# A chunk's running sum ordered behind the present step of the RWKV scan, and the solution's values copied on chip instead of loaded again

## The chip, the cores and the metric

The kernel runs on one core of a Trainium2 chip. The metric is the device time of one launch, in microseconds (us). Five engines work from instruction queues of their own, each strictly in its order: TensorE (PE, with its weight loads as PEld), VectorE (DVE), ScalarE (ACT), GpSimd (POOL) and SyncE (SP, which here only issues DMAs).

## The reference, cut to what matters

Two layers of a trunk with three token mixers (RWKV-7 in both directions, latent attention, a Fourier mix), gates and a gated ConvFFN, on 512 latent and 256 context tokens of width 1024. The change lies in the RWKV recurrence, six heads of 64 by 64 state in each of two directions:

```python
def _rwkv_step(S, inp):
    r, w, k, v, a, b = inp
    sa = jnp.einsum('bhij,bhj->bhi', S, a)
    S = S * w[:, :, None, :] + sa[..., None] * b[:, :, None, :] + v[..., None] * k[:, :, None, :]
    return S, jnp.einsum('bhij,bhj->bhi', S, r)
...
for d in range(2):
    S_c, y_c = rwkv_scan(S0, scan_inputs(prep_c), d == 1)
    _, y_l = rwkv_scan(S_c, scan_inputs(prep_l), d == 1)
```

## The kernel before, in words

`rwkv_scan` (L942) runs once a layer, in 12 steps. A step takes one chunk of 64 tokens of each direction, so that 12 pairs of head and direction lie in one tile. Two things are done for a chunk n.

- `prep(n, X)` (L1002) needs no state. It takes the tile X, which `load(n)` (L985) fetched from DRAM with four DMAs on SP (two of `rwx`, two of `rws`; two buffers of X, `XB`). On DVE the running sum `cum` of the log decays (L1006), on ACT five exponentials of it (L1013 to L1017), on DVE the scaled operands BK (L1024, L1026) and AR (L1027, L1030; half of L1030 on POOL), on PE the products in the banks "f" and their masking to MA and MY on DVE (L1048), a transposed copy Bn (L1057), and then `inverse` (L1063): a unit triangular matrix is inverted in eight rounds, in each of which PE multiplies 32 by 32 blocks (`quads`, bank "i") and DVE or ACT (L1091 to L1139) makes the next round's operand. The result is the tile TT. Last, POOL copies AR's rows into MA (L1060), which the step reads as WA. TT, MA, MY, Bn and AR have three buffers (`DEEP`).
- `step(n, SV, UV, pk)` (L1142) is the recurrence. PE multiplies the state SV by WA ("st<-SV,MA"), DVE copies the result to Rh (L1153), PE multiplies by TT ("st<-Rh,TT"), DVE and ACT copy that into half of the rows of UV (L1160, L1161), PE multiplies by Bn ("st<-UV,Bn"), DVE scales it to St (L1173), and DVE and POOL add it to the decayed state Sg to give the next SV (L1175; Sg is POOL's, L1166). The outputs y are products of SV and UV with AR and MY.

The other rows of SV and of UV hold the chunk's values v. They are the same numbers in the same rows, and each tile gets them from DRAM by four DMAs of 48 KB on SP: SV in `state` (L973, three buffers), UV in `values` (L995, three buffers, `UB`).

PE's other work in this stage is the background: gate projections ("w" at L688, evacuated by ACT at L693 from a single bank) and modulation vectors ("a" at L258). `bg.after` (L781) places a bounded piece of it behind each group of the scan's matmuls, so that PE has something to do while DVE and ACT make the next operand. What is left of the gate projections in layer 0 goes into the following stages.

The order on each engine is set at build time by a scheduler (`SCHED`, L79) from the program's order, priorities and `tc.issue_after(x)`, which places the instructions inside behind x. In the program step(n) is followed by prep(n + 2), and load(n + 3) stands ahead of step(n) (L1210 to L1217).

Of the kernel before, what the change touches and what calls it, by code (L numbers as in the profile page):

```python
# [11 lines left out]
F32 = mybir.dt.float32  # L12
# [3 lines left out]
ALU = mybir.AluOpType  # L16
# [49 lines left out]
MFILL, AFILL = 2.5, 0.3  # L66
FIRST = ((12, 2.0), (8, 3.0))
MORE = False
XB, UB = 2, 3
MID = (False, True)  # L70
FILL = (1.0, 0.8)
PRE = (12.0, 24.0)
# [10 lines left out]
def hybrid_backbone_kernel(ctx: ExitStack, tc: tile.TileContext, A, out, dbg=None):  # L83
    nc = tc.nc
    V, S, P, TE = nc.vector, nc.scalar, nc.gpsimd, nc.tensor
# [29 lines left out]
    def C(name, n=None):  # L115
        o = COFF[name]
        w = dict(CCOLS)[name] if n is None else n
        return cst[:, o:o + w]
# [45 lines left out]
    v_tok = dram.tile([T, 2, 3, 64], F32, name="v_tok")  # L164
# [777 lines left out]
    def rwkv_scan(l, last, pool, fill):  # L942

        hs = (slice(0, 64), slice(64, 128))
# [27 lines left out]

        def state(n):  # L973

            SV = pool.tile([128, 2, 6, 64], F32, tag="SV", name="SV", bufs=3)
            for d, c in enumerate(chunks(n)):
                for p in range(2):
                    nc.sync.dma_start(out=SV[hs[1 - p], p, 3 * d:3 * d + 3, :], in_=v_tok[c * 64:c * 64 + 64, p])
            return SV


        def chunks(n):
            return (8 + n, 11 - n) if n < 4 else (n - 4, 11 - n)

        def load(n):  # L985
            ch = chunks(n)
            need_y = not (last and n < 4)
            X = pool.tile([128, 5, 2, 192], F32, tag="X", name="X", bufs=XB)
            for d in range(2):
                w = 2 if need_y else 1  # L990
                nc.sync.dma_start(out=X[:, 2:5, d], in_=rwx[d, ch[d]].rearrange("p w c t -> p w (c t)"))
                nc.sync.dma_start(out=X[:, 0:w, d], in_=rws[ch[d], :, 0:w].rearrange("p w c t -> p w (c t)"))
            return X

        def values(n):  # L995
            UV = pool.tile([128, 2, 6, 64], F32, tag="UV", name="UV", bufs=UB)
            for d, c in enumerate(chunks(n)):
                for p in range(2):
                    nc.sync.dma_start(out=UV[hs[1 - p], p, 3 * d:3 * d + 3, :], in_=v_tok[c * 64:c * 64 + 64, p])
            return UV  # L1000

        def prep(n, X):  # L1002
            need_y = not (last and n < 4)
            w = 128 if need_y else 64
            cum = pool.tile([128, 2, 192], F32, tag="cum", name="cum", bufs=1)
            V.tensor_tensor_scan(out=cum.rearrange("p d x -> p (d x)"), data0=C("seq"), data1=X[:, 4].rearrange("p d x -> p (d x)"),  # L1006
                                 initial=0.0, op0=ALU.mult, op1=ALU.add)
            G = Gs[n % 2]
            I = X[:, 4]
            gc = pool.tile([128, 6], F32, tag="gc", name="gc", bufs=4)  # L1010
            c = 0.5 * DECAY_C
            c3 = lambda t: t.rearrange("p (c t) -> p c t", t=64)
            S.activation(out=I[:, 0], in_=cum[:, 0], func=AF.Exp, scale=c)  # L1013
            S.activation(out=c3(I[:, 1])[:, :, ::-1], in_=c3(cum[:, 1]), func=AF.Exp, scale=c)
            S.activation(out=G[:, 0:198].rearrange("p (c x) -> p c x", x=66)[:, :, 1:65], in_=c3(cum[:, 0]), func=AF.Exp, scale=-c)
            S.activation(out=G[:, 199:397].rearrange("p (c x) -> p c x", x=66)[:, :, 63::-1], in_=c3(cum[:, 1]), func=AF.Exp, scale=-c)
            S.activation(out=gc.unsqueeze(2), in_=cum.rearrange("p d (c t) -> p (d c) t", t=64)[:, :, 63:64], func=AF.Exp, scale=-c)  # L1017
            gv = lambda o, st: G[:, o:o + 2 * st].rearrange("p (d y) -> p d y", y=st)[:, :, 0:198].rearrange("p d (c x) -> p d c x", x=66)[:, :, :, 0:64]
            Gex, Gin = gv(0, 200), gv(1, 198)
            x4 = lambda i: X[:, i].rearrange("p d (c t) -> p d c t", t=64)  # L1020
            AR = ARs[n % DEEP]
            BK = pool.tile([128, 6, 192], F32, tag="BK", name="BK", bufs=1)
            u4 = lambda t: t.rearrange("p (d c) x -> p d c x", d=2)
            V.tensor_tensor(out=u4(BK)[:, :, :, 0:64], in0=x4(2), in1=I.rearrange("p d (c t) -> p d c t", t=64), op=ALU.mult)  # L1024
            S.activation(out=BK[:, :, 128:192], in_=BK[:, :, 0:64], func=AF.Copy)
            V.tensor_tensor(out=u4(BK)[:, :, :, 64:128], in0=x4(3), in1=I.rearrange("p d (c t) -> p d c t", t=64), op=ALU.mult)  # L1026
            V.tensor_tensor(out=u4(AR[:, :, 1, :]), in0=x4(0), in1=Gex, op=ALU.mult)  # L1027
            if need_y:
                for p, e in enumerate((V, P)):
                    e.tensor_tensor(out=u4(AR[:, :, 2 - 2 * p, :])[hs[p]], in0=x4(1)[hs[p]], in1=Gin[hs[p]], op=ALU.mult)  # L1030

            MA = pool.tile([128, 2, 6, 64], F32, tag="MA", name="MA", bufs=DEEP)
            MY = pool.tile([128, 2, 6, 64], F32, tag="MY", name="MY", bufs=DEEP)
            for d in range(2):
                pp = [pss("f")[:, 0:384].rearrange("p (u t) -> p u t", t=128) for _ in range(2)]
                run = Run()
                for ct in range(3):
                    u = 3 * d + ct
                    for p in (1, 0):
                        a = slice(1 - p, 3 - p) if need_y else slice(1, 2)  # L1040
                        i = run(TE.matmul, pp[p][:, ct, 0:w], lhsT=BK[hs[p], u, 64 * p:64 * p + 128], rhs=AR[hs[p], u, a, :].rearrange("p s x -> p (s x)"), start=True, stop=True)
                if MORE:
                    fill(i)
                for i, M in ((0, MA), (1, MY))[:w // 64]:
                    mb = mask[:, d, 64 * i:64 * i + 64].unsqueeze(1).to_broadcast([128, 3, 64])
                    for p in range(2):
                        o = 64 * (i ^ p) if need_y else 0
                        V.tensor_tensor(out=M[:, p, 3 * d:3 * d + 3], in0=pp[p][:, :, o:o + 64], in1=mb, op=ALU.mult)  # L1048
            Bn = pool.tile([128, 2, 6, 64], F32, tag="Bn", name="Bn", bufs=DEEP)
            pp, run = [pss("f"), pss("f")], Run()  # L1050
            for u in range(6):
                for p in range(2):
                    i = run(TE.transpose, pp[p][:, u * 64:(u + 1) * 64], BK[hs[p], u, 64 * p:64 * p + 128], ident[hs[p], hs[p]])
            if MORE:
                fill(i)
            for p in range(2):
                S.activation(out=Bn[:, p].rearrange("p u j -> p (u j)"), in_=pp[p][:, 0:384], func=AF.Copy)  # L1057
            TT = inverse(n, MA)
            for p in range(2):
                P.tensor_copy(MA[hs[p], p], AR[hs[p], :, 1, :])  # L1060
            return AR, MY, Bn, TT, gc, MA
# [79 lines left out]

        def step(n, SV, UV, pk):  # L1142
            AR, MY, Bn, TT, gc, WA = pk
# [3 lines left out]
            ps, run = pss("st"), Run()  # L1147
            for u in range(6):
                for p in range(2):
                    i = run(TE.matmul, ps[hs[p], u * 64:(u + 1) * 64], lhsT=WA[:, p, u, :], rhs=SV[:, p, u, :], start=True, stop=True)  # L1150
            fill(i)
            Rh = pool.tile([128, 384], F32, tag="Rh", name="Rh", bufs=1)
            V.tensor_copy(Rh, ps[:, 0:384])  # L1153
            ps, run = pss("st"), Run()
            for u in range(6):
                for p in range(2):
# [5 lines left out]
            if n < 11:  # L1162
# [4 lines left out]
                ps, run = pss("st"), Run()  # L1167
# [8 lines left out]
            if need_y:  # L1176
                ps = pss("st")
# [20 lines left out]
                    S.dma_start(out=y_dram[d, :, :, ch[d] * 64:ch[d] * 64 + 64].rearrange("c p t -> p c t"), in_=yt[:, d])  # L1198
            return SV1

        ld = [load(0), load(1)]
        SV = state(0)
        for p in range(2):
            P.memset(SV[hs[p], p], 0.0)
        uv = [values(0), values(1)]
        pk = [prep(0, ld[0])]
        ld.append(load(2))
        uv.append(values(2))
        pk.append(prep(1, ld[1]))
        for n in range(12):  # L1210
            if n + 3 < 12:
                ld.append(load(n + 3))
            SV = step(n, SV, uv[n], pk[n])
            if n + 3 < 12:
                uv.append(values(n + 3))
            if n + 2 < 12:
                pk.append(prep(n + 2, ld[n + 2]))  # L1217

    def rwkv_out(l, last, pool, fill):

# [39 lines left out]
    for k in range(KD):  # L1260
        x = xp.tile([128, T], F32, name=f"x{k}")
# [24 lines left out]
    for l in range(DEPTH):  # L1286
# [8 lines left out]
        with ExitStack():  # L1295
# [28 lines left out]
            def fill(us=MFILL):  # L1324
                bg.run(us)
# [27 lines left out]
        with ExitStack() as es:  # L1353
            for c in range(8):
                x = xp.tile([128, T], F32, name=f"x{c}")
# [4 lines left out]
            with ExitStack() as e2:  # L1360
                tp = near(e2, l, f"mt{l}")
                for c in range(8):
                    acc = None
                    for x in (2, 1, 0):
                        t = tp.tile([128, T], F32, tag=f"t{x}", name=f"t{x}", bufs=2)
                        nc.sync.dma_start(out=t[:, ar], in_=t_dram[x, c][:, ar])
                        ps = dense(A[("w_ba", "w_bb", "w_bc")[x]][l, c], len(yX[x][0]), yX[x][0], yX[x][1], streams)
# [169 lines left out]
```

## Time and profile before

| | us |
|---|---|
| median of 3 runs (lowest to highest) | 2766.99 (2765.91 to 2770.1) |
| the profiled execution, its own time | 2763.33 |
| its span, first to last instruction | 2761.6 |
| PE busy | 2580.6 (93%) |
| DVE, ACT, POOL busy | 1474.6 (53%), 1076.6 (39%), 209.7 (8%) |
| mean granted TensorE clock | 0.975 |
| scan of layer 0, from its first cum | about 211 to 590 |
| scan of layer 1 | about 1789 to 2121 |

A share of busy time is a mean over stages. The two scans together are 711 of the 2761.6 us, and the change acts only there.

### The profile page before, as it was taken

The numbers are of one execution on the slowest core, as the hardware profiler recorded it, in microseconds if no ns is written. First come the engines' busy times: TensorE is split into PE (matmuls) and PEld (weight loads), VectorE is DVE, ScalarE is ACT, GpSimd is POOL, SyncE is SP. The second block draws the span as 40 slices with busy tenths as digits, with TensorE's granted clock in tenths as the row PEclk, the third lists the DMA queues.
The fourth block names the chain that finished last, engine by engine and source line by source line (L and its number), as shares of the span: only waits on it lengthen the run. The fifth ranks groups of instructions, "written<-read, shape, count | busy, mean of one in ns | idle before, by whom it ended". The sixth has DMA issues, their size and how long they took to land.

```text
span 2761.6 us, 56820 instructions
## 1 busy us (share of the span) xinstructions
PE 2580.6 (93%) x24016; PEld 2062.0 (75%) x24016; DVE 1474.6 (53%) x2965; ACT 1076.6 (39%) x1914; POOL 209.7 (8%) x268
## 2 busy tenths in 40 slices
PE   6998998997899999999999999998898899899999
PEld 4866776775776887888888877666666668878778
DVE  6444545434446765445354564445564768755455
ACT  4353333332445253222222344544343564533333
POOL 0121121100010000000000001302220000000000
PEclk9999998998999999999999999999999999999999
DMA  6365443356441641221212254765444417333334
GB/s 264 93 176 173 132 137 108 119 190 205 133 139 42 183 122 48 60 69 55 68 49 74 61 170 109 234 196 154 134 134 148 130 50 220 108 92 90 98 95 123
DMA packets 168947, 344.18 MB, mean 125 GB/s; under 512 B 33618, under 2 KB 84436, under 8 KB 168692
## 3 DMA queue, kind: packets, MB, share of 16 engines
q1 hardware_dynamic: 132532, 278.66, 32.5%
q0 software_dynamic: 10944, 36.58, 5.0%
q10 hardware_dynamic: 25216, 25.30, 2.7%
q8 instruction: 190, 3.11, 0.5%
q14 instruction: 65, 0.53, 0.1%
HBM read 278.60 MB, written 61.87 MB: 123 GB/s over the span
## 4 chain that ended last, share of the span: by engine, by line
PE 67%; DMA 5%; DVE 5%; ACT 2%; issue 2%; SPq 1%; ACTq 0%; POOL 0%; DVEq 0%; POOLq 0%
PE mm L220 44%; PE w L688 9%; PE mm L567 2%; DMA wr<-in_w_ada 2%; PE r L595 2%; PE s L584 1%; PE st L957 1%; PE i L957 1%; DVE wl L184 1%; PE mm L394 1%; DMA X<-rwx 1%; PE a L258 1%; PE w L258 1%; PE s L871 1%; DMA raw<-m_dram 1%
## 5 line engine op out<-in xcount | busy, mean ns | idle before, releaser
L183 ACT ACTIVATE wh<-wr 128x1024 fp32r<-128x1024 f32 (+4 forms) x334 | 302.0, 906 | 373.7 <-PE mm L220 272.1
L184 DVE TENSOR_TENSOR wl<-wr,wh 128x1024 fp32r<-128x1024 f32 (+3 forms) x332 | 342.8, 1034 | 59.4 <-ACT wh L183 56.9
L220 PE MATMUL mm<-fH,wh 128*128 128x512 f32 (+1 forms) x1072 | 223.9, 357 | 10.3 <-DVE ab L232 7.2
L231 DVE SCALAR_TENSOR_TENSOR ab<-mm,prm,ab 128x511 f32<-128x511 f32 (+1 forms) x132 | 86.8, 658 | 262.3 <-ACT ab L229 262.3
L220 PE MATMUL mm<-fH,wl 128*128 128x512 f32 (+1 forms) x1072 | 220.3, 353 | 0.0
L220 PE MATMUL mm<-fL,wh 128*128 128x512 f32 (+1 forms) x1072 | 219.6, 352 | 0.0
L688 PE MATMUL w<-hH,wh 128*128 128x512 f32 (+1 forms) x760 | 189.0, 385 | 22.4 <-ACT gt L693 21.0
L220 PEld LDWEIGHTS mm<-fH,wh 128*128 128x128 f32 x1072 | 178.1, 191 | 41.7 <-issue 6.4
L220 PEld LDWEIGHTS mm<-fH,wl 128*128 128x128 f32 x1072 | 175.8, 189 | 29.6
L220 PEld LDWEIGHTS mm<-fL,wh 128*128 128x128 f32 x1072 | 175.4, 188 | 29.5
L688 PE MATMUL w<-hL,wh 128*128 128x512 f32 (+1 forms) x760 | 184.4, 374 | 0.0
L220 PE MATMUL mm<-gH,wh 128*128 128x512 f32 (+1 forms) x568 | 174.5, 346 | 10.0 <-ACT wh L183 4.4
L688 PE MATMUL w<-hH,wl 128*128 128x512 f32 (+1 forms) x760 | 174.6, 364 | 2.7 <-issue 2.7
L220 PE MATMUL mm<-gH,wl 128*128 128x512 f32 (+1 forms) x568 | 175.4, 348 | 1.1 <-DVE wl L184 0.9
L688 PEld LDWEIGHTS w<-hH,wh 128*128 128x128 f32 x760 | 128.6, 197 | 63.2 <-ACT gt L693 29.6
L1255 DVE SCALAR_TENSOR_TENSOR x<-mm,mod,x 128x256 f32<-128x256 f32 (+1 forms) x136 | 80.1, 607 | 173.1 <-PE mm L220 172.2
L220 PE MATMUL mm<-gL,wh 128*128 128x512 f32 (+1 forms) x568 | 171.5, 343 | 0.0
L229 ACT ACTIVATE ab<-mm,prm 128x768 f32<-128x768 f32 (+1 forms) x88 | 69.9, 795 | 217.9 <-PE mm L220 217.9
L688 PEld LDWEIGHTS w<-hL,wh 128*128 128x128 f32 x760 | 128.6, 195 | 25.1 <-issue 4.1
L688 PEld LDWEIGHTS w<-hH,wl 128*128 128x128 f32 x760 | 128.1, 192 | 24.7 <-issue 3.3
L220 PEld LDWEIGHTS mm<-gH,wh 128*128 128x128 f32 x568 | 97.1, 188 | 29.6 <-ACT wh L183 10.4
L693 ACT ACTIVATE gt<-w 128x512 f32<-128x512 f32 x99 | 51.4, 519 | 161.7 <-PE w L688 143.6
(387 smaller groups left out, 4649.8 us busy)
## 6 DMA issues: line engine op xcount, KB each, us to landing
wr<-in_w_up SPq DMA_DIRECT2D x88, 512.0 KB
wr<-in_w_ada SPq DMA_DIRECT2D x80, 512.0 KB
wr<-in_w_g SPq DMA_DIRECT2D x48, 512.0 KB
wr<-in_w_out SPq DMA_DIRECT2D x32, 512.0 KB
wr<-in_w_dn SPq DMA_DIRECT2D x48, 320.0 KB
X<-rwx SPq DMA_DIRECT2D x48, 288.0 KB
wr<-in_w_rw SPq DMA_DIRECT2D x24, 512.0 KB
wr<-in_w_dn SPq DMA_DIRECT2D x32, 384.0 KB
```

What stands on the lines that cost most here:

```text
L183: S.activation(out=H, in_=raw, func=AF.Copy)
L184: e.tensor_tensor(out=L, in0=raw, in1=H.bitcast(F32), op=ALU.subtract)
L220: TE.matmul(ps[:, a:b], lhsT=W[:, k, :], rhs=X[k][:, a:b], start=(k == 0 and n == 0), stop=(k == kt - 1 and n == 2))
L229: S.activation(out=o[:, a:b], in_=ps[:, a:b], func=AF.Identity, scale=w[1])
L231: V.scalar_tensor_tensor(out=o[:, a + 1:b], in0=ps[:, a:b - 1], scalar=w[0], in1=o[:, a + 1:b], op0=ALU.mult, op1=ALU.add)
L258: TE.matmul(ps[32 * i:32 * i + 32], lhsT=cs32[:, k, :], rhs=w[:, k - k0], start=(k < 4), stop=(k >= 4))
L567: TE.matmul(ps[:, a:b], lhsT=qT[:, h, t * 128:(t + 1) * 128], rhs=kT[:, h, a:b], start=True, stop=True)
L595: TE.matmul(po[64 * p:64 * p + 64, 0:128], lhsT=Vn[:, j, h * 64:(h + 1) * 64], rhs=pts[p][:, j * 128:(j + 1) * 128], start=(j == kts[0]), ...
L688: TE.matmul(ps, lhsT=w[:, k, :], rhs=X[k][:, a:b], start=(k == 0 and n == 0), stop=(k == 7 and n == 2))
L693: S.activation(out=t[:, a:b], in_=ps, func=AF.Tanh if it[0] == "g" else AF.Copy, scale=0.5 if it[0] == "g" else 1.0)
L957: self.i = f(*a, **k)
L1255: V.scalar_tensor_tensor(out=x[:, a:b], in0=ps[:, a:b], scalar=mod[l][:, j, c, s:s + 1], in1=x[:, a:b], op0=ALU.mult, op1=ALU.add)
```

## The change

The running sum of prep(n + 2) is placed behind the copy Rh of step n. UV is no longer loaded: `values(SV)` copies the value rows out of SV's tile with two POOL copies of 64 partitions by 384. UV goes from three buffers to two, SV from three to four.

```diff
-XB, UB = 2, 3
+XB, UB = 2, 2
...
-            SV = pool.tile([128, 2, 6, 64], F32, tag="SV", name="SV", bufs=3)
+            SV = pool.tile([128, 2, 6, 64], F32, tag="SV", name="SV", bufs=4)
...
-        def values(n):
+        def values(SV):
             UV = pool.tile([128, 2, 6, 64], F32, tag="UV", name="UV", bufs=UB)
-            for d, c in enumerate(chunks(n)):
-                for p in range(2):
-                    nc.sync.dma_start(out=UV[hs[1 - p], p, 3 * d:3 * d + 3, :], in_=v_tok[c * 64:c * 64 + 64, p])
+            for p in range(2):
+                P.tensor_copy(UV[hs[1 - p], p], SV[hs[1 - p], p])
             return UV
 
-        def prep(n, X):
+        def prep(n, X, behind=None):
...
-            V.tensor_tensor_scan(out=cum.rearrange("p d x -> p (d x)"), data0=C("seq"), data1=X[:, 4].rearrange("p d x -> p (d x)"),
-                                 initial=0.0, op0=ALU.mult, op1=ALU.add)
+            with tc.issue_after(behind.ins) if behind else ExitStack():
+                V.tensor_tensor_scan(out=cum.rearrange("p d x -> p (d x)"), data0=C("seq"), data1=X[:, 4].rearrange("p d x -> p (d x)"),
+                                     initial=0.0, op0=ALU.mult, op1=ALU.add)
...
-            V.tensor_copy(Rh, ps[:, 0:384])
+            rhs[0] = V.tensor_copy(Rh, ps[:, 0:384])
...
-        uv = [values(0), values(1)]
         pk = [prep(0, ld[0])]
         ld.append(load(2))
-        uv.append(values(2))
         pk.append(prep(1, ld[1]))
         for n in range(12):
             if n + 3 < 12:
                 ld.append(load(n + 3))
-            SV = step(n, SV, uv[n], pk[n])
-            if n + 3 < 12:
-                uv.append(values(n + 3))
+            SV = step(n, SV, values(SV), pk[n])
             if n + 2 < 12:
-                pk.append(prep(n + 2, ld[n + 2]))
+                pk.append(prep(n + 2, ld[n + 2], rhs[0]))
```

The scheduler gives the scan's instructions another order. Three places show it.

**DVE, layer 0, around the copy Rh of step 5.** L1006 is the running sum, L1153 the copy Rh. Before, the sum in this piece is that of chunk 9:

```order
L1114 STREAM_TRANSPOSE iXt<-iX 128x192
L1100 STREAM_TRANSPOSE iD4t<-i_4761 128x192
L1101 TENSOR_TENSOR iX<-i_4761,iDX 128x192
L1006 SCALAR_TENSOR_TENSOR cum<-cst,X 128x384
L1027 TENSOR_TENSOR AR_1879<-X,G_1873 128x6x64
L1048 TENSOR_TENSOR MA<-f,cst 128x192
...
L1103 TENSOR_TENSOR iNX<-i_4794,iX 128x6x32
...
L1153 COPY Rh<-st 128x384
```

Of the change, where the sum behind Rh of step 5 is that of chunk 7:

```order
L1097 STREAM_TRANSPOSE iD2t<-i_4699 128x192
L1153 COPY Rh<-st 128x384
L1006 SCALAR_TENSOR_TENSOR cum<-cst,X 128x384
L1100 STREAM_TRANSPOSE iD4t<-i_4736 128x192
L1101 TENSOR_TENSOR iX<-i_4736,iDX 128x192
L1024 TENSOR_TENSOR BK<-X 128x6x64
```

Before, up to five sums stand ahead of the Rh of their time; in the change each of chunks 2 to 11 stands directly behind an Rh, in both layers.

**SP, layer 0, loads of one step.** L978 loads SV, L999 loads UV, L991 and L992 load X, L191 and L245 are the background's weights. Before:

```order
L978 DMA SV<-v_tok 64x192
L999 DMA UV<-v_tok 64x192 x4
L991 DMA X<-rwx 128x3x192
L992 DMA X<-rws 128x2x192
L991 DMA X<-rwx 128x3x192
L992 DMA X<-rws 128x2x192
L978 DMA SV<-v_tok 64x192 x3
```

Of the change:

```order
L991 DMA X<-rwx 128x3x192
L992 DMA X<-rws 128x2x192
L991 DMA X<-rwx 128x3x192
L992 DMA X<-rws 128x2x192
L191 DMA wr<-in_w_g 128x1024
L978 DMA SV<-v_tok 64x192 x4
```

The 96 loads of UV are gone from SP's queue, and the four DMAs of an X no longer stand behind them.

**PE, layer 0, step 1, from the second to the third product of the step.** Before:

```order
L957 MATMUL st<-Rh,TT_1871 64x64 x11
L954 MATMUL i_3002<-iXt,iE 32x32
L957 MATMUL i_3002<-iXt,iE 32x32 x23
L688 MATMUL w<-hL_153,wh 128x512
L688 MATMUL w<-hL_154,wh 128x512
L688 MATMUL w<-hL_155,wh 128x512
L688 MATMUL w<-hL_156,wh 128x512
L954 MATMUL f<-AR_1877,BK 128x128
L957 MATMUL f<-AR_1877,BK 128x128 x5
L954 MATMUL st<-UV,Bn 64x64
```

Of the change:

```order
L957 MATMUL st<-Rh,TT_1871 64x64 x11
L954 MATMUL f<-cst,BK 128x64
L957 MATMUL f<-cst,BK 128x64 x11
L954 MATMUL st<-UV,Bn 64x64
```

Here less work of PE stands between the two products. The total of PE's work in the scans is the same.

## Rows read from the trace of the kernel before

**Rows 1.** Windows: the two scans (busy us, instructions in brackets).
```profile
core 0: us, PE busy (x) PEld busy (x) DVE busy (x) ACT busy (x) POOL busy (x), PEclk, DMA share, GB/s
211.00:590.00 379.00, 345.29 (x6925) 271.36 (x6924) 178.81 (x423) 133.75 (x340) 65.90 (x83) 0.95 0.44 130
1789.00:2121.00 332.00, 304.59 (x6368) 224.17 (x6367) 179.36 (x422) 132.17 (x326) 57.48 (x65) 0.97 0.51 154
```
**Rows 2.** Waits of PE, first scan (us in total, times, longest).
```profile
PE w L688 <- ACT gt L693: 11.9, 4, 7.0
PE i L954 <- DVE iDt L1091: 4.4, 1, 4.4
PE i L954 <- DVE iX L1101: 4.1, 2, 3.3
PE i L954 <- ACT iQ L1125: 2.6, 1, 2.6
...
PE f L954 <- DVE MY L1048: 2.1, 2, 1.5
PE i L954 <- DVE iX L1111: 1.4, 1, 1.4
```
**Rows 3.** Waits of PE, second scan.
```profile
PE w L688 <- ACT gt L693: 6.0, 3, 5.7
PE i L954 <- DVE iXt L1114: 5.4, 4, 3.2
PE a L258 <- DMA wr<-in_w_ada: 4.4, 3, 2.5
PE i L954 <- ACT iQ L1125: 2.1, 1, 2.1
```
**Rows 4.** The running sum's line L1006, both scans: what DVE waited for.
```profile
  DMA X<-rwx: 84.5, 19
```
**Rows 5.** Timeline, first scan: start, duration, engine, line, count, idle before.
```profile
391.68 1.65 PE L688 MATMUL w<-hH,wh 128*128 128x512 f32 x6 [2.41 <-ACT gt L693]
...
406.02 3.13 SPq L999 DMA_DIRECT2D UV<-v_tok  x4
...
409.26 0.55 SPq L991 DMA_DIRECT2D X<-rwx  x1
...
415.78 0.96 DVE L1006 TENSOR_TENSOR_SCAN cum<-cst,X 128x384 f32<-128x384 f32 x1 [7.07 <-DMA X<-rwx]
...
416.82 0.36 ACT L1013 ACTIVATE X<-cum 128x192 f32<-128x192 f32 x1 [7.99 <-DVE cum L1006]
...
420.78 3.67 PE L688 MATMUL w<-hH,wh 128*128 128x512 f32 x8 [7.01 <-ACT gt L693]
```
**Rows 6.** Windows: one stretch at the lower granted clock, and the sum of six.
```profile
417.38:424.20 6.82, 3.42 (x8) 2.75 (x9) 3.79 (x12) 2.49 (x7) 0.00 (x0) 0.50 0.36 102
...
sum 44.36, PE 33.52 PEld 23.79 DVE 24.13 ACT 19.86 POOL 4.67; mean PE 5.59 PEld 3.96 DVE 4.02 ACT 3.31 POOL 0.78
```
**Rows 7.** Groups of PE by shape, 262 to 362 us (busy us, mean ns).
```profile
L688 PE MATMUL w<-hH,wl 128*128 128x512 f32 x45 | 12.7, 416 | 0.0
L957 PE MATMUL f<-AR,BK 64*128 64x128 f32 x70 | 6.5, 282 | 0.0
L957 PE MATMUL i<-iX,iD2t 32*32 32x32 f32 x184 | 2.6, 194 | 0.1
L957 PE MATMUL f<-cst,BK 64*128 64x64 f32 x33 | 1.7, 227 | 0.0
```
**Rows 8.** Tile UV: three of its instructions (ns min/median/max).
```profile
L999 SPq DMA_DIRECT2D UV<-v_tok x96: 444/593/1980, 230.2 to 2060.9; - x96
L1160 DVE COPY UV<-st x24: 510/549/550, 289.9 to 2118.8; 64x384 f32<-64x384 f32 x24
L1161 ACT ACTIVATE UV<-st x24: 485/485/488, 290.5 to 2119.3; 64x384 f32<-64x384 f32 x24
```
**Rows 9.** POOL's present copies of this size (line L1060).
```profile
L1060 POOL COPY MA<-AR x48: 496/505/722, 275.1 to 2112.3; 64x384 f32<-64x384 f32 x48
```
**Rows 10.** DVE's half of the multiply L1030; POOL does the other half.
```profile
L1030 DVE TENSOR_TENSOR AR<-X,G x20: 542/1167/1364, 229.2 to 2057.9; 64x384 f32<-64x384 f32 x20
```

More of the change, by code (lines that the diff above doesn't have):

```diff
@@ L1199, in step @@
             return SV1
+        rhs = [None]
         ld = [load(0), load(1)]
```

## The prediction

> **What bounds the kernel now.** I read the windows first, to see which engine has no room in the stage that the change touches. In the two scans PE is busy 345.3 of 379.0 us and 304.6 of 332.0 us, VectorE and ScalarE about half of it, GpSimd a sixth [rows 1]. PE bounds the scans, and its total work there is the same in both kernels. So the change can pay only through PE's idle time, 33.7 and 27.4 us, and through stretches at the lower clock.
>
> Then the waits of PE, to see what that idle time is. Single long waits make up most of it, not many short ones: in the first scan 7.0 us on the evacuation gt, 4.4 on iDt, 4.1 on iX, 2.6 on iQ [rows 2]; in the second 5.7 on gt, 3.2 on iXt, 2.1 on iQ [rows 3]. These name different producers, so the next question is what held the producers. The running sum's line answers it: DVE stood idle 84.5 us in 19 waits for the DMA of X before that one instruction [rows 4]. DVE works in order, so everything queued behind the sum stands too.
>
> One stall in full: SP issues four loads of UV from 406.02 us, which take it 3.13 us, and only then the first part of X, at 409.26 [rows 5]. The sum starts at 415.78, 6.5 us after that issue, and DVE has been idle for 7.07 us. ScalarE waits 7.99 us for the sum at the head of its own queue; the evacuation gt, which needs nothing from the sum, stands behind that exponential, and PE waits 7.01 us for gt. The sum is that of chunk 9, needed four steps later. Nothing was urgent but the place in the queue.
>
> **The change, part by part.**
>
> *The sum behind Rh.* The sum of chunk n + 2 now follows Rh of step n, in both scans. X of that chunk goes into the buffer that prep n has finished with nearly two steps earlier; a step lasts up to 379 / 12 = 31.6 us [rows 1], and a load takes 6.5 us from issue to use [rows 5]. So I expect X to be there, and the waits of [rows 4] to fall to nearly none. Of PE's waits I count as removed those whose producer stood behind such a sum: 7.0 + 2.4 on gt [rows 2, 5], 4.4, 4.1 and 2.6 [rows 2], that is 20.5 us; in the second scan 5.7 + 3.2 + 2.1 = 11.0 us [rows 3]. Together **31.5 us**.
>
> *The clock.* Six stretches at a granted clock of 0.50 (the lower level, 1.2 GHz) begin in or right behind these stalls; before each PE stood idle. In them PE was busy 33.5 us [rows 6]. A gate product of 512 columns took 3.67 / 8 = 0.46 us there [rows 5], against 12.7 / 45 = 0.28 us in a stretch at almost full clock [rows 7], so 39% of those 33.5 us would go: **13 us**. Bounds: nothing, if other stalls of that size appear, and 17 (half).
>
> *UV no longer loaded.* 96 DMA issues of 0.593 us leave SP's queue [rows 8], 57 us of SP time. SP is not the bound; what can gain is what stood behind them: the X (counted above) and the weights for w_ada, for which PE waited 4.4 us in the second scan [rows 3]. Between 0 and 4.4 I take **2 us** off.
>
> *The copies on GpSimd.* 48 copies of 64 by 384 at 0.505 us [rows 9] make 24 us of GpSimd, busy 123 of 711 us [rows 1]. They stand behind Sg and ahead of the product that reads UV by the step's first two products, so no one waits for them directly. Their price is that they may hold DVE. The trace shows such a price: DVE's half of L1030 takes 0.542 us at best and 1.167 in the median, when GpSimd's half runs beside it [rows 10]. Bounds: 0, and 48 x 0.505 = 24 us if every copy held DVE for its whole length and every hold reached PE. DVE is busy half of the time [rows 1] and most holds vanish behind PE's queued work, so I take **2 us** on. The rule that speaks against this edit is in the Trainium skill, SBUF — State Buffer, section on the two separate sides: DVE and GpSimd share a port pair under an exclusive lock, held for the whole instruction, when GpSimd reads SBUF and DVE has two SBUF inputs. The row of L1030 agrees with it. By that rule alone the edit would cost up to those 24 us, and the sum would be about nothing.
>
> *The shorter lead.* This is the term that gives back. Before, up to five sums ran ahead of the step; now two. The scheduler has less of other chunks' work to put between two dependent products, and PE's order shows it. I call it a link when a group of PE's products needs what DVE or ACT make of the group before: seven between the eight rounds of each inversion, Rh, and UV; there are 214 in the two scans. A link's cover is PE's work queued between the two groups. In the piece of step 1 shown above it was 24 products of 32 columns, four gate products and six of BK, about 0.7 + 1.1 + 1.1 = 2.9 us at the prices of [rows 7] (of f and i two records make one product); now it is twelve transposes, 12 x 0.05 = 0.6 us. Yet the link needs a DVE copy and an ACT copy one after the other, 0.549 + 0.485 us [rows 8], and the signals between. Done for all 214, with other shapes priced from the same view, the count of links with less than 2 us of cover goes from 11 to 42.
>
> What does a link need? At least the 1.03 us above. If each needed 2.2 us, the covers before would fall short by 9.9 us in all. PE's short waits on DVE and ACT, those that are no stall behind a sum (2.1 on MY, 1.4 on iX [rows 2], 5.4 - 3.2 on iXt [rows 3], and smaller ones), come to about 10 us. So 2.2 us is the need that the trace bears out, and at 2.2 the covers of the change fall short by 31.9 us. Difference: **22 us** given back. Bounds: 4 at a need of 1.5 us, 72 at 3.5.
>
> *Buffers.* UV with two and SV with four buffers change no wait that the trace shows: UV's second buffer is free a step earlier than needed, and SV's loads can only go earlier. Cost nothing; if that cover failed, POOL's copy would wait for the outputs of step n - 2, which PE does before step n.
>
> **The sum**: -31.5 - 13 - 2 + 2 + 22 = -22.5 us against the profiled execution's own 2763.3 us, so 2740.8. The median of the runs, 2767.0, stands 3.7 us above that execution, so I forecast **2744.5 us**.
>
> **The rivals.**
>
> 1. *The lead is too short (slower).* Two steps of lead leave the inversion's rounds no slack: a DVE or ACT operand that is late by its place in the queue now reaches PE, in the rounds of L1091 to L1114 above all. Its price is the shortfall by a larger need: at 3.5 us per link 164.1 against 92.1 us, 72 more, hence -46.5 + 2 + 72 = +27.5 and **2794.5 us**. It decides from a need of about 2.8 us, where the shortfall eats all gains. For it: 42 thin links against 11. Against it: many of DVE's long answers came from the sums that now wait for nothing, and the short waits of [rows 2, 3] fit 2.2.
>
> 2. *GpSimd's copies hold DVE.* All 48 reach PE: -46.5 + 22 + 24 = -0.5, **2766.5 us**. For it: L1030's median is twice its minimum [rows 10]. Against it: two copies a step against some 35 DVE instructions (423 / 12 [rows 1]), and covers that are mostly over 2 us.
>
> 3. *X is late all the same.* The X loads still share SP's queue with SV's, which wait for the end of a step. If that made X late, the sum would block DVE right behind Rh, with the copy UV and St of the same step behind it: the stalls stay and the thin links come on top, up to 2767 + 22 = **2789 us**. Against it: nearly two steps of slack for a load of 6.5 us.
>
> **How the numbers follow.** A measurement of this kernel can tell about 0.2% (5.5 us) from no change. Forecast 0.70, all of it faster; rival 1 0.13, slower; rival 2 0.10, no change; rival 3 0.04, slower; a gain that a later stage makes up, 0.03, no change. So faster 0.70, same 0.13, slower 0.17. The low end takes the smallest give-back: -46.5 + 4 is 2724.5, and waits too small to be listed may add some, so 2718. The high end goes beyond no change to a need of 3 us, 2776; above it lies most of rival 1 and half of rival 3. About 0.16 is left out above and 0.04 below.
>
> **What the profile of the change would show.** Right: the line of the sum has hardly any wait for X's DMA; ScalarE's wait for the sum falls from 7.99 us to about 1; the long waits of PE on gt, iDt and iX are gone, and fewer stretches at 0.50 lie in the scans; PE's waits are more in number and mostly under 2 us. Wrong, by rival 1: waits of PE on iXt, iX, iQ and iDt that sum to more than 60 us. By rival 2: DVE's L1027 and L1048 get longer medians, with GpSimd's copies beside them. By rival 3: waits for X stay at the sum. If PE's idle time falls but the span does not, a later stage makes it up, and I have misread what bounds it.

## The result, and the profile after

| | before | after |
|---|---|---|
| median of the runs, us | 2767.47 (4 runs, 2765.91 to 2770.1) | 2730.75 (4 runs, 2727.55 to 2736.8) |
| the profiled execution, its span | 2761.6 | 2735.0 |

The ratio is 0.9865 (95% interval 0.9848 to 0.9882): 36.7 us faster, where 22.5 were forecast. The profiled execution of the change, 2736.8 us, is the longest of its four; between the two profiles 26.6 us of span lie.

First the windows, which now follow each kernel's own scans (from its first sum to its last output) and the stretches before, between and behind them. Of the change:

```profile
...
216.50:573.50 357.00, 337.64 (x6904) 265.89 (x6902) 175.94 (x423) 132.26 (x337) 78.26 (x102) 0.98 0.43 128
573.50:1763.20 1189.70, 1141.48 (x6491) 935.63 (x6492) 617.14 (x1161) 442.94 (x675) 43.14 (x63) 0.98 0.37 112
1763.20:2095.50 332.30, 316.09 (x6426) 230.30 (x6425) 177.33 (x421) 131.68 (x327) 68.28 (x89) 0.97 0.48 146
2095.50:2735.00 639.50, 600.59 (x3186) 491.39 (x3186) 392.58 (x733) 274.79 (x438) 9.92 (x19) 0.97 0.38 115
sum 2735.00, PE 2585.12 PEld 2061.64 DVE 1471.11 ACT 1076.90 POOL 235.32; mean PE 517.02 PEld 412.33 DVE 294.22 ACT 215.38 POOL 47.06
```

The same cut of the kernel before (it stands here because [rows 1] has other bounds):

```profile
...
214.40:589.60 375.20, 341.49 (x6907) 268.16 (x6906) 178.81 (x423) 132.58 (x338) 64.52 (x80) 0.95 0.43 128
589.60:1789.50 1199.90, 1145.41 (x6493) 939.98 (x6494) 615.84 (x1159) 442.46 (x675) 43.03 (x63) 0.98 0.36 111
1789.50:2126.20 336.70, 309.29 (x6424) 227.71 (x6422) 179.36 (x422) 131.67 (x326) 57.48 (x65) 0.97 0.50 151
2126.20:2761.60 635.40, 596.55 (x3186) 488.59 (x3186) 392.52 (x733) 274.87 (x438) 9.89 (x19) 0.98 0.38 115
sum 2761.60, PE 2580.59 PEld 2062.05 DVE 1474.61 ACT 1076.60 POOL 209.72; mean PE 516.12 PEld 412.41 DVE 294.92 ACT 215.32 POOL 41.94
```

The first scan became 18.2 us shorter, the second 4.4, the stretch between them 10.2; the stretches ahead of the scans and behind them became 2.1 and 4.1 longer. What went is idle time of PE, length less busy time. In the two scans it was 33.7 + 27.4 = 61.1 us and is 19.4 + 16.2 = 35.6, that is 25.5 us less; over the whole span it fell from 181.0 to 149.9. PE's busy time did not fall at all (2580.6 to 2585.1): it is 3.9 us less in the first scan, where less of PE's work ran at the lower clock (15.2 us, before 26.0), but 6.8 us more in the second.

The line of the sum, both scans of the change, answers [rows 4]:

```profile
L1006 DVE TENSOR_TENSOR_SCAN cum<-cst,X x24: 935/948/959, 216.5 to 2035.2; 128x384 f32<-128x384 f32 x24
...
  DMA X<-rwx: 10.1, 3
who waited for it (us, times):
  ACT X L1013: 50.7, 20
```

DVE's 84.5 us in 19 waits are 10.1 in 3. In both numbers are the waits ahead of the first sum of each scan, which has no Rh to stand behind: 6.8 and 12.5 us before, 7.8 and 1.9 of the change. So the other sums lost some 65 us of waits, and none that stands behind an Rh waits for X now. PE's waits in the first scan of the change answer [rows 2]:

```profile
PE i L957 <- issue: 6.1, 6, 1.7
PE i L954 <- DVE iDt L1091: 4.3, 4, 1.5
PE w L688 <- ACT gt L693: 3.1, 3, 2.0
PE f L954 <- DVE MY L1048: 2.1, 2, 1.5
PE st L954 <- DVE UV L1160: 1.9, 1, 1.9
```

And in the second scan, for [rows 3]:

```profile
PE a L258 <- DMA wr<-in_w_ada: 4.6, 2, 4.2
PE f L954 <- DVE AR L1027: 4.0, 2, 3.6
PE i L954 <- DVE iXt L1114: 1.8, 2, 1.3
PE i L954 <- DVE iX L1101: 1.3, 2, 0.7
PE i L954 <- ACT iQ L1125: 1.2, 3, 0.6
```

In the first scan the longest is 2.0 us where it was 7.0. In the second two longer ones are left: 4.2 us on the w_ada weights, for which PE waited before too, and 3.6 on AR, which is not among [rows 3].

One thing did not come as I said. The place of the 7.07 us stall of [rows 5] has a counterpart, in which X is there and the sum starts at once behind Rh. From the change's timeline of DVE and ACT:

```profile
416.25 0.56 DVE L1153 COPY Rh<-st 128x384 f32<-128x384 f32 x1 [4.35 <-PE st L957]
416.72 0.95 DVE L1006 TENSOR_TENSOR_SCAN cum<-cst,X 128x384 f32<-128x384 f32 x1
417.76 0.37 ACT L1013 ACTIVATE X<-cum 128x192 f32<-128x192 f32 x1 [5.50 <-DVE cum L1006]
```

ScalarE still waits 5.50 us for this sum, not 1: DVE now stands at Rh, which needs PE's first product of the step, and the sum behind it. Over both scans ScalarE's wait fell from 90.2 us (the kernel before, same line) to 50.7. It no longer shows at PE: no wait of PE in this scan is over 2.0 us. Nor did PE's waits become more in number, as I had said: by the full lists they were 41 in the two scans and are 38.

A third of the lower-clock time went, and much of the rest moved. The stretches at a granted 0.50 within the scans, by windows, of the change:

```profile
...
330.30:333.80 3.50, 3.50 (x81) 3.28 (x81) 0.24 (x1) 1.58 (x3) 0.94 (x2) 0.51 0.02 5
1985.80:1992.60 6.80, 6.15 (x90) 5.05 (x92) 3.23 (x10) 0.94 (x3) 0.00 (x0) 0.50 0.66 204
...
sum 34.40, PE 31.33 PEld 21.52 DVE 11.31 ACT 9.47 POOL 7.53; mean PE 4.48 PEld 3.07 DVE 1.62 ACT 1.35 POOL 1.08
```

There are seven, 34.4 us with PE busy 31.3 of them. The kernel before has eight in its scans:

```profile
sum 51.30, PE 40.41 PEld 28.69 DVE 28.63 ACT 21.85 POOL 7.35; mean PE 5.05 PEld 3.59 DVE 3.58 ACT 2.73 POOL 0.92
```

So 9.1 us of work at the lower clock went, net, not 33.5. What PE did ahead of a stretch differs: ahead of that at 1985.8 us it waited the 3.6 us on AR, ahead of another at 2074.5 the 4.2 us on w_ada, but ahead of that at 330.3 it only stood 1.7 us (the longest of the issue row above).

### The profile page after: what moved, and what is told of

It reads as the page before. It is cut to its first block, busy times and chain, and to the rows that moved or that the text cites. A ratio compares the mean times of both kernels' runs of the same rounds, so it can differ in the third digit from the quotient of the medians.

```text
span 2735.0 us, 56808 instructions
## 1 busy us (share of the span) xinstructions
PE 2585.1 (95%) x24016; PEld 2061.6 (75%) x24016; DVE 1471.1 (54%) x2965; ACT 1076.9 (39%) x1914; POOL 235.3 (9%) x316
## 4 chain that ended last, share of the span: by engine, by line
PE 85%; DMA 5%; DVE 5%; ACT 3%; issue 2%; SPq 0%; ACTq 0%; DVEq 0%; POOL 0%; POOLq 0%
PE mm L220 47%; PE w L688 15%; PE i L957 2%; PE st L957 2%; PE mm L567 2%; DMA wr<-in_w_ada 2%; PE r L595 2%; PE a L258 2%; PE mm L394 2%; PE s L584 1%; PE s L871 1%; PE f L957 1%; DVE wl L184 1%; PE i L954 1%; PE f L954 1%
## 5 line engine op out<-in xcount | busy, mean ns | idle before, releaser
L220 PE MATMUL mm<-fH,wh 128*128 128x512 f32 (+1 forms) x1072 | 224.7, 358 | 10.2 <-DVE ab L232 7.1
L688 PEld LDWEIGHTS w<-hH,wh 128*128 128x128 f32 x760 | 124.6, 191 | 44.5 <-ACT gt L693 13.4
L220 PEld LDWEIGHTS mm<-gH,wl 128*128 128x128 f32 x568 | 97.4, 188 | 17.8 <-DVE wl L184 3.9
```

The costliest lines, as they stand in the source:

```text
L220: TE.matmul(ps[:, a:b], lhsT=W[:, k, :], rhs=X[k][:, a:b], start=(k == 0 and n == 0), stop=(k == kt - 1 and n == 2))
L688: TE.matmul(ps, lhsT=w[:, k, :], rhs=X[k][:, a:b], start=(k == 0 and n == 0), stop=(k == 7 and n == 2))
```

## The experiments

All ratios are to the kernel before on the same chip. Two runs whose intervals overlap widely are not told apart.

**Which half of the change does it?** The kernel before with the ordering alone, UV still loaded:

```diff
+            with tc.issue_after(behind.ins) if behind else ExitStack():
...
-            V.tensor_copy(Rh, ps[:, 0:384])
+            rhs[0] = V.tensor_copy(Rh, ps[:, 0:384])
...
-                pk.append(prep(n + 2, ld[n + 2]))
+                pk.append(prep(n + 2, ld[n + 2], rhs[0]))
```

> The kernel before with the sums ordered behind Rh, and nothing else: UV is still loaded. Theory (the sum no longer stops VectorE's queue): nearly all of the change's 36.7 us stays, so 2728 to 2738 us; the sum's waits for X, 84.5 us before and 10.1 in the change, are below 25; the lower-clock time falls to about the change's 120 us. Rival (the loads of UV taken out of SyncE's queue are what pays): the 96 issues still stand ahead of X, so most of the gain is gone, 2752 us or more.

Measured: ratio 0.9897 (0.9877 to 0.9916), 2732.7 us against 2760.8. And the change without the ordering:

```diff
-                pk.append(prep(n + 2, ld[n + 2], rhs[0]))
+                pk.append(prep(n + 2, ld[n + 2]))
```

> The change without the ordering: GpSimd copies the values, no load of UV, the sums stand where the scheduler puts them. Theory: up to five sums still run ahead of the step and wait for X in a buffer that is not free yet, 60 to 85 us of such waits at the sum's line; so 2758 to 2768 us, of which minus 2 for the loads and plus 2 for the copies. Rival (the loads): X comes earlier, the waits fall below 30 us, 2735 to 2745 us.

Measured: ratio 1.0009 (0.9995 to 1.0023). The line of the sum in the second of these:

```profile
L1006 DVE TENSOR_TENSOR_SCAN cum<-cst,X x24: 951/958/959, 214.6 to 2028.3; 128x384 f32<-128x384 f32 x24
...
  DMA X<-rwx: 72.9, 21
```

and in the one with the ordering alone, where one line more stands ahead:

```profile
L1007 DVE TENSOR_TENSOR_SCAN cum<-cst,X x24: 939/948/960, 214.8 to 2037.6; 128x384 f32<-128x384 f32 x24
...
  DMA X<-rwx: 18.6, 2
```

Both came as the theory had it; the 18.6 us are the first sums of the two scans. The scans by windows, first of the ordering alone:

```profile
...
214.80:570.60 355.80, 336.75 (x6909) 267.36 (x6908) 176.82 (x423) 133.19 (x339) 67.50 (x82) 0.98 0.46 136
...
1763.20:2093.90 330.70, 313.33 (x6429) 229.35 (x6427) 177.08 (x422) 132.44 (x326) 56.57 (x65) 0.98 0.51 155
```

and of the copies alone:

```profile
...
214.60:580.90 366.30, 335.61 (x6908) 267.21 (x6907) 179.29 (x423) 132.32 (x338) 78.63 (x105) 0.96 0.41 125
...
1777.70:2123.30 345.60, 314.66 (x6426) 230.37 (x6425) 175.71 (x421) 132.50 (x327) 69.53 (x89) 0.96 0.46 141
```

PE's idle time in the scans was 61.1 us before and is 35.6 in the change; it is 36.4 with the ordering alone and 61.6 with the copies alone. The ordering carries the gain; without it, the 96 loads taken off SyncE's queue neither shorten the waits for X by much (84.5 to 72.9 us) nor the time. Without the ordering the long waits of PE stay, only at other places. First scan of the copies alone:

```profile
PE i L954 <- DVE iX L1101: 9.4, 4, 3.3
PE f L954 <- DVE MY L1048: 5.7, 2, 4.2
PE i L954 <- DVE iXt L1114: 5.1, 1, 5.1
```

**Did the shorter lead cost 22 us?** Each sum one step earlier, three chunks ahead, the rest as in the change. By my count from the order of PE's queue, made as in the prediction, the links with under 2 us of cover then number 12, much as before the change (11), and not 42. It ran twice, the second time beside the change.

```diff
-            rhs[0] = V.tensor_copy(Rh, ps[:, 0:384])
+            rhs.append(V.tensor_copy(Rh, ps[:, 0:384]))
...
-                pk.append(prep(n + 2, ld[n + 2], rhs[0]))
+                pk.append(prep(n + 2, ld[n + 2], rhs[-2]))
```

> The change with each sum placed behind Rh one step earlier, that is three chunks ahead instead of two. By the order of TensorE's queue, links with under 2 us of cover go from the change's 42 back to 12 (the kernel before: 11), and X's load has about one step of slack left instead of two. If thin links cost the change the 22 us that the forecast gave them: 2708 to 2718 us. If they cost little, since a link now needs less than 2.2 us: within 5 us of the change, 2725 to 2736. If one step is too short for X: waits for X at the sum of 30 us or more, and 2740 or more.

Measured: ratio 0.9868 (0.9848 to 0.9888), 2726.2 us.

> The change itself, unaltered, beside the next three on one chip, since the earlier four ran on another chip than it did. Both theories: a ratio of 0.985 to 0.988 to the kernel before.

Measured: ratio 0.9869 (0.9845 to 0.9893), 2731.95 us; the change repeats itself on another chip.

> The change with each sum one step earlier (three chunks ahead), again, on the chip of the change. If thin links cost the change 22 us: 18 us or more below the change. If they cost little: between 8 us below and 3 above. In the profiles its first scan was 10 us shorter than the change's (347.0 against 357.0), so I expect 4 to 8 us below.

Measured: ratio 0.9842 (0.9816 to 0.9868), 2722.4 us, 9.5 below the change: somewhat more than the 8 that I had allowed, far from 18, and with intervals that overlap. Taken together, 0.9868 and 0.9842 against 0.9865 and 0.9869: thicker covers give between nothing and 10 us. The scans of the second run, by windows:

```profile
...
215.60:566.20 350.60, 331.65 (x6908) 263.25 (x6907) 180.00 (x423) 132.36 (x339) 77.45 (x105) 0.98 0.44 131
...
1759.40:2083.20 323.80, 310.28 (x6428) 228.38 (x6427) 177.19 (x422) 132.10 (x327) 72.18 (x89) 0.98 0.49 151
```

and of the change beside it:

```profile
215.40:569.10 353.70, 335.96 (x6906) 265.07 (x6906) 175.50 (x423) 132.28 (x338) 78.50 (x104) 0.98 0.43 129
1760.50:2092.90 332.40, 316.33 (x6427) 229.47 (x6425) 177.65 (x421) 131.94 (x326) 68.25 (x89) 0.97 0.48 146
```

PE's idle time in the scans is 19.0 + 13.5 = 32.5 us with thick covers and 17.7 + 16.1 = 33.8 with thin ones: the 30 thin links cost 1.3 us of idle time. The two scans are 11.7 us shorter with thick covers all the same, since PE's busy time is 10.4 us less. Less of it is at the lower clock (20.8 against 26.8 us), which at the prediction's 39% is 2.3 us; the rest is not explained.

My expectation was wrong in one point: X's load does not lose a step of slack, since its buffer comes free a step earlier too. The sum waits for X only at the starts of the scans.

One such wait is the sum of chunk 2, which nothing orders there. I put it behind the first Rh as well.

```diff
-                pk.append(prep(n + 2, ld[n + 2], rhs[-2]))
+                pk.append(prep(n + 2, ld[n + 2], rhs[max(1, n)]))
```

> Sums three chunks ahead as before, but the sum of chunk 2, which no Rh held back there and which waited 3.3 to 3.9 us for X in front of the first two inversions, goes behind the first Rh with that of chunk 3. If that unordered sum cost the start (the first Rh came at 285.1 and 289.3 us against 278.4 and 281.0 in the change): 2 to 12 us below the run with three chunks ahead, a ratio of 0.980 to 0.9835. If not: 0.984 to 0.987.

Measured: ratio 0.987 (0.9855 to 0.9886). The first Rh came at 280.0 us instead of 285.1 and 289.3, as thought, but the time did not follow: a start that is earlier by 5 us was worth nothing that can be measured.

Then four chunks ahead:

```diff
-                pk.append(prep(n + 2, ld[n + 2], rhs[max(1, n)]))
+                pk.append(prep(n + 2, ld[n + 2], rhs[max(1, n - 1)]))
```

> Sums four chunks ahead: those of chunks 2, 3 and 4 behind the first Rh, each later one behind the Rh two steps before the change's place. Theory (a sum may run ahead as long as X is there): X for the third sum in a row cannot be there, since its buffer is only just free, so one wait of 5 to 7 us at each scan's start, later none; covers as with three ahead, so within 5 us of that, ratio 0.980 to 0.988. Rival (any run ahead beyond three brings the stalls back): waits for X over 40 us and a ratio above 0.992.

Measured: ratio 0.9932 (0.9916 to 0.9948), so half of the gain is lost. The line of the sum:

```profile
  DMA X<-rwx: 36.9, 8
```

In the second scan four sums behind the first Rh wait 1.8 to 3.8 us each for X, two of them at 1895 and 1949 us, far from the start. Of the 36.9 us, 18.3 stand ahead of the first sums of the scans (6.8 and 11.5), much as with three ahead in the first of its runs (6.6 and 11.6); the other 18.6 are six waits of sums behind an Rh, where my theory allowed one at each start. The two named reach PE: it waits 2.6 us on iX until 1898.4 and 2.8 on iXt until 1950.7 us, and a stretch at a granted 0.50 begins at 1897.9 and at 1952.6. In the two scans PE's idle time is hardly more than in the version before this one (35.1 against 34.3 us), but its work at the lower clock is (34.2 against 15.1). The profiled execution is the fastest of its six, 9 us below their median, so a part of the loss is not in view. With two buffers, then, X's arrival is what stops the sums from running further ahead; a third buffer of X was not tried.

**Are the copies worth anything?** Three chunks ahead with the ordered start as above, but in the kernel before, which loads UV (and has three buffers of UV and of SV):

```diff
-            V.tensor_copy(Rh, ps[:, 0:384])
+            rhs.append(V.tensor_copy(Rh, ps[:, 0:384]))
...
-                pk.append(prep(n + 2, ld[n + 2]))
+                pk.append(prep(n + 2, ld[n + 2], rhs[max(1, n)]))
```

> The first of these three with UV loaded again instead of copied, that is the kernel before with the sums ordered three chunks ahead. If the copies are worth nothing beside the loads: within 4 us of it (0.0015 in the ratio). If the loads on SyncE delay X and the weights, or the copies' freedom pays, as the order alone (0.9897 against 0.9865 and 0.9869 for the change) hints: 5 to 10 us above it.

Measured, beside the copies on one chip: 2727.7 us, ratio 0.9878 (0.9862 to 0.9894), against 2724.3 and 0.987. With two chunks ahead the ratios were 0.9897 (loads) and 0.9865 and 0.9869 (copies). By these two pairs the copies are worth 2 to 8 us, but the intervals overlap in both, so it is not told from nothing.

**What do GpSimd's copies cost?** Each copy done twice; then each made by ScalarE.

```diff
-                P.tensor_copy(UV[hs[1 - p], p], SV[hs[1 - p], p])
+                for _ in range(2):
+                    P.tensor_copy(UV[hs[1 - p], p], SV[hs[1 - p], p])
```

> The change with each of GpSimd's 48 copies of the values done twice, 24 us more of GpSimd. Theory (nobody waits for these copies, and what they hold of VectorE is hidden): within 4 us of the change, 2727 to 2735. Rival (each copy holds VectorE and the hold reaches TensorE): 12 to 24 us more, 2743 to 2755, and L1027 and L1048 longer in the median than the change's 1.291 and 0.348 us.

Measured: ratio 0.992 (0.9901 to 0.9939), 2740.7 us, between the two ranges; and neither of the two lines grew to speak of (1.294 and 0.349 us, each one line further down). Again beside the change:

> GpSimd's copies of the values done twice, again, on the chip of the change. If the copies cost what the first look suggests (its ratio was 0.0055 above that of the change's own runs), 10 to 18 us above the change. If that was the chip or chance: within 4 us.

Measured: 2742.9 us, 11 above the change, so neither the chip nor chance; ratio 0.992 (0.9895 to 0.9946). DVE is busy 17.7 us more in the scans (370.8 against 353.2). But most of this is not the price of a copy. The row that grew most is that of the step's last add, whose two halves DVE and GpSimd make side by side. Doubled copies (one line more stands ahead here):

```profile
L1176 POOL TENSOR_TENSOR SV<-St,Sg x22: 992/997/1373, 292.3 to 2077.0; 64x384 f32<-64x384 f32 x22
L1176 DVE TENSOR_TENSOR SV<-St,Sg x22: 550/1384/1400, 292.3 to 2077.1; 64x384 f32<-64x384 f32 x22
```

The change:

```profile
L1175 DVE TENSOR_TENSOR SV<-St,Sg x22: 549/551/1367, 294.2 to 2065.7; 64x384 f32<-64x384 f32 x22
L1175 POOL TENSOR_TENSOR SV<-St,Sg x22: 994/1369/1392, 294.3 to 2065.7; 64x384 f32<-64x384 f32 x22
```

The half that is first keeps its 0.55 or 1.00 us, and the other takes 1.37 to 1.38. The doubled copies turned the two round in 17 more of the 22 steps, which holds DVE 0.83 us longer in each: DVE's 22 adds take 27.4 us in all, against 13.4 in the change, so 14.0 of the 17.7. That this is also what made the kernel slower is likely and not shown. So what one copy costs was not measured by doubling it.

```diff
-                P.tensor_copy(UV[hs[1 - p], p], SV[hs[1 - p], p])
+                S.activation(out=UV[hs[1 - p], p], in_=SV[hs[1 - p], p], func=AF.Copy)
```

> The change with the 48 copies of the values made by ScalarE instead of GpSimd, 48 x 0.485 = 23 us of ScalarE. If GpSimd's copies hold VectorE and TensorE waits for it, their removal gains: 10 to 20 us below the change. If they are hidden, the copies now stand in the queue of an engine that the links need: 0 to 10 us above the change.

Measured: 2740.6 us, 8.6 above the change; ratio 0.991 (0.9886 to 0.9934). The time alone tells little: the copies took 0.522 us each on ScalarE, 25 us in all, which may hide a gain. DVE's busy time in the two scans tells more. It is 353.6 us here and 353.9 with the ordering alone, both without a copy on GpSimd, and 353.3 and 353.2 in the two profiles of the change. So GpSimd's copies do not lengthen DVE's work by anything that shows.

**A version that uses the finding.** Three chunks ahead, and both halves of that add on DVE:

```diff
-                for p, e in enumerate((V, P)):
+                for p, e in enumerate((V, V)):
                     e.tensor_tensor(out=SV1[hs[p], p], in0=St[hs[p]], in1=Sg[hs[p]], op=ALU.add)
```

> Sums three chunks ahead, and both halves of the last add of a step (L1175) on VectorE instead of one half on GpSimd. Side by side the pair takes about 1.37 us from the first start to the last end, since one half waits for the other (0.55 against 1.37 us in the change, 1.00 against 1.39 with the copies doubled). Theory: one after the other on VectorE they take 2 x 0.55 = 1.10 us, 0.27 us less in each of 22 links, up to 6 us; at 0.55 us more of VectorE a step. So 0 to 6 us below three chunks ahead, ratio 0.982 to 0.987. Rival (VectorE's queue is the scarcer): the added 12 us of VectorE come back as waits, 3 to 8 us above, ratio 0.988 to 0.990.

Measured: ratio 0.9899 (0.9876 to 0.9922); the 44 adds take 0.554 us in the median, as thought, but the ratio is above that of three chunks ahead (0.9868, 0.9842), as the rival had it, though its interval overlaps that of the first. PE's idle time in the two scans is 39.5 us, against 31.8 and 32.5 there. By median, three chunks ahead is the fastest of all; whether it beats the change stays open.

## Why the prediction was right, point by point

- **The sum behind Rh, 31.5 us of PE's waits.** Right. The long waits named are gone (on iDt 4.3 us are left, in four waits of at most 1.5), and PE's idle time in the scans fell by 25.5 us net of what came anew (35.6 left; 33.8 in the repeat). The mechanism is shown by the two halves: the order alone gives 0.9897 and 36.4 us of idle time, the copies alone 1.0009 and 61.6. The 84.5 us of [rows 4] were read too high: 19.3 of them stand ahead of the scans.
- **The clock, 13 us.** In the two scans of the profiled pair too large: 9.1 us of busy time at the lower clock went, not 33.5, and at my 39% that is 3.5 us. New stretches took the place of old ones. I had taken the long stalls behind a sum to be the only thing that brings one; two of the new ones stand behind other long waits, on AR and on w_ada, and that at 330.3 us behind a stop of 1.7 us. But the pair shows less than the runs do. Its granted clock rose from 0.975 to 0.978, and the other three executions of the change have 0.981 and 0.982. Beside each other on one chip, the clock is 0.970 to 0.975 in eleven runs of the kernel before and 0.979 to 0.983 in five of the change, in the mean 0.973 and 0.980. If all that is missing from 1 is time at 0.50, that is about 149 and 107 us, and the 42 us less are worth at most 16 at 39%, by this estimate. The ordering alone raises the clock too (0.974 to 0.980 in the mean), the copies alone do not (0.973). So the mechanism holds, and how much of the 13 us came is not settled.
- **UV's loads, 2 us off, and GpSimd's copies, 2 us on.** Not refuted: together they are worth up to 8 us, not separable from nothing. The wait on w_ada stayed (4.4 to 4.6 us), so that part of the gain did not come.
- **The shorter lead, 22 us given back.** This is the step that failed. Thin links there are (42 by my count of PE's order), but a link does not need 2.2 us. I had fitted 2.2 to the short waits of the kernel before, in which DVE and ACT were late because a sum stood in their queues; the change takes that lateness away too. Followed in the traces from the end of PE's group to the end of DVE's and ACT's answer, 119 links a scan (the step's last add counted too), the need fell from 1.67 and 1.88 us in the mean to 1.21 and 1.49, and the links above 3 us from 32 to 13. The run with thick covers prices the thin ones at 1.3 us of idle time, and at 10 us of run time at most. For the idle time in the scans I had forecast -31.5 + 22 = -9.5 us, and it fell by 25.5: 16 us too little.
- **The sum.** In the profiled pair the scans became 22.6 us shorter, beside a forecast of 22.5, and that is luck: PE's busy time in them was to fall by the clock's 13 us and rose by 2.9, 16 us too much, which cancels the 16 us of idle time. Of the 36.7 us between the medians, another 4 lie outside the scans, and 10 come from where the two profiled executions stand among their runs.
- **Rival 1** did not come: PE's waits on iXt, iX, iQ and iDt are about 10 us, not 60. **Rival 3** neither: X is there. At four chunks ahead it does appear, with 18.6 us behind an Rh.
- **Rival 2** did not come, though its sign seemed to: L1027's median went from 0.550 to 1.291 us. The cause is not the copies. DVE's half of L1030 fell from 1.167 us [rows 10] to 0.542: DVE now issues L1027 while GpSimd does its half of L1030, and the wait has moved from one line to the other. The ordering alone, with no copy on GpSimd, shows the same 1.288 us (one line further down; the rows stand below). DVE's busy time in the scans even fell, 358.2 to 353.3 us. The Trainium skill, SBUF — State Buffer, section on the two separate sides, has the one that starts first keep the shared port pair for its whole instruction; who loses changes with the order. Here the rows agree in who waits, but not on a full block: that would be 0.55 + 1.00 = 1.55 us for the step's last add, and its pair takes 1.41 to 1.42 (last section).

The rows of rival 2, of the change:

```profile
L1027 DVE TENSOR_TENSOR AR<-X,G x24: 537/1291/1339, 230.3 to 2037.8; 128x384 f32<-128x384 f32 x24
```

```profile
L1030 DVE TENSOR_TENSOR AR<-X,G x20: 540/542/1278, 230.7 to 2039.0; 64x384 f32<-64x384 f32 x20
```

and of the ordering alone:

```profile
L1028 DVE TENSOR_TENSOR AR<-X,G x24: 539/1288/1337, 229.7 to 2040.2; 128x384 f32<-128x384 f32 x24
```

- **What stays open.** Why PE's busy time in the second scan rose by 6.8 us with the same instructions: the lower-clock stretches there do not tell it, and no group of PE's products accounts for it alone. And the 10.2 us between the scans, where the change touches nothing: in the other runs with the ordering that stretch was 1.1 to 8.5 us shorter than before, and 3.1 with the copies alone. I did not try to tell a cause from chance there.

## What to carry to other kernels

Work that is not urgent must not stand at the head of an in-order queue with a load that has not landed: the cost is not its own wait but everything behind it, and it shows at PE under other names. Place such work behind an instruction of the critical chain that comes after the load is sure to be there; a little too early gave half of the gain back here. And a need that was fitted to the waits of the old kernel contains the very fault that the change removes, so it must not be used to price what is left.

## What the runs showed of the hardware that I had not expected

Two instructions that DVE and GpSimd start within 0.1 us of each other, each with two inputs in SBUF, do not slow each other evenly. The first to start keeps its own time and the other waits. From the timeline of the change and then of the doubled copies:

```profile
294.21 0.55 DVE L1175 TENSOR_TENSOR SV<-St,Sg 64x384 f32<-64x384 f32 x1
294.26 1.37 POOL L1175 TENSOR_TENSOR SV<-St,Sg 64x384 f32<-64x384 f32 x1 [1.89 <-issue]
```

```profile
292.33 1.00 POOL L1176 TENSOR_TENSOR SV<-St,Sg 64x384 f32<-64x384 f32 x1 [1.83 <-DVE St L1174]
292.34 1.40 DVE L1176 TENSOR_TENSOR SV<-St,Sg 64x384 f32<-64x384 f32 x1
```

In the second pair a lead of 0.01 us decides. The pair ends 1.41 to 1.42 us after its first start in either case (not 1.37, as I had put it): 0.13 to 0.14 less than 0.55 + 1.00 one after the other. Two halves one after the other on DVE are 2 x 0.55 = 1.11 us by the last experiment's 0.554. So for the pair itself splitting the add between the two engines gains no time, though with DVE first it spares DVE one half of it. Which engine is held turns here on a few hundredths of a microsecond, and an edit elsewhere (the doubled copies) shifted that.
